# A hybrid decoder layer on one core: the third token chunk's down projection of the first MLP group placed ahead, the second chunk's sums ordered by use, and the first norm's constant moved

## The chip, the cores and the metric

One core of a Trainium2 chip runs the whole layer. The core has a matrix engine (TensorE, PE in the rows; PEld is its weight load), three element-wise engines (VectorE, DVE; ScalarE, ACT; GpSimd, POOL) and a queue that issues transfers (SyncE, SP). The metric is the device time of one execution in microseconds (us), as the median of several runs.

## What is computed

The layer takes 1024 prompt tokens and 8 sampled tokens of width 1024. It norms them, projects them, runs a gated delta rule and a sparse attention, merges the two and adds the residual (h). The MLP behind it takes about two fifths of the time. What matters here, cut from the reference:

```
def rms_norm(x, g):
    y = xf * rsqrt(mean(xf * xf) + EPS);  return y * g
...
xn = rms_norm(x, norm1_g);  ... = split(xn @ w_in)
mix = sigmoid(ga) * (oa @ w_out_a) + sigmoid(gb) * (ob @ w_out_b)
h  = x + mix @ w_o
hn = rms_norm(h, norm2_g)
y  = h + square(relu(hn @ w_up)) @ w_down
```

## The kernel before

Tokens lie along the free dimension in three chunks: 0 and 1 of 384 tokens, 2 of 264 (256 prompt tokens and the 8 samples). `CN` holds the widths. Features lie on the 128 partitions, in 8 slices of 128. Every float32 factor is split into a high and a low part (`split`: ScalarE copies the high part, VectorE or GpSimd subtracts for the low part), and each product is three matmuls, high by high, low by high, high by low.

The program is written as generators ("chains") that `flow.run` interleaves by events (`ev_...`); then a scheduler of the framework puts the instructions of each engine in a fixed order. An engine takes its instructions strictly in that order. All operations are issued through one helper, so every row of the profile shows line 86, and one goes by tile names.

**Start.** `x_chain` loads a tile of 128 tokens (`xt`), gets 1/rms with three small Newton steps on VectorE (`rs`, `ru`), and multiplies tile, 1/rms and the weight `g1`. The Newton steps are written without their usual halves, which leaves a factor of -8192 in `rs`; one GpSimd operation on the 128x1024 weight `g1` takes it out. TensorE then transposes the tile (`ptx`), and `xn` gets the high and low parts. Products `pk` with the weight `wk` (8 slices, split by ScalarE and GpSimd) and `pqi` with `wiq` follow.

**Merge.** For chunks in the order 2, 0 (`FIRST`) and then 1 (`REST`), the attention result `ob` is projected and gated into `mix`, and `mix @ w_o` is added to the residual `hT[j]` in 8 steps (`pdn<-mix,wc`). After each step `part` squares the new slice and adds it to `ssq[j]`.

**Second norm.** `norm_chain` turns the sums of squares into 1/rms (`rs[j]`): a matmul with ones (`pn`), then `rsqrt` (ten VectorE operations, on tiles 264 or 384 wide for chunks 2 and 0; for chunk 1 on 3 columns, which three transposes `pb` widen again). Chunk 2 becomes `hn`, normed and split. Chunks 0 and 1 go through a product scheme that needs seven products of 2x2 blocks instead of eight: with b11, b21 the halves of chunk 0 and b12, b22 those of chunk 1, it forms t1 = b12 - b11, t2 = b22 - t1, t3 = b22 - b12, t4 = b21 - t2 (tiles `bt`; `b22` too is needed in parts), and like sums of weight blocks (`pair`).

**MLP.** `mlp_chain` runs 8 groups `g` of 512 hidden features. A group has products up (`pc` for chunk 2, `pp` for chunks 0 and 1), a squared ReLU (`out`, tiles `r`, `u`), and products down (`pdn<-u,wc`), added to `hT` in 8 steps for chunks 1, 0, 2. In the first group (`g == 0`) all `pc` and the products with b11 and b21 stand ahead of `ev_n[1]`, the end of chunk 1's norm; the products with the `bt` tiles and all of down stand behind it. Weight blocks (128x512, tiles `wc`) are loaded, split and handed out by `ahead` in the order of the list `todo`. `cur["spare"]` names a further raw buffer for every third block.

Of the kernel before, what the change touches and what calls it, by code (L numbers as in the profile page):

```python
# [8 lines left out]
F32 = mybir.dt.float32  # L9
# [7 lines left out]
P = 128  # L17
# [111 lines left out]
def program(ctx, tc, I, O, dbg=None, upto=99):  # L129
# [321 lines left out]
    def mixers():  # L451
# [49 lines left out]
        def x_chain():  # L501
# [12 lines left out]
            G.tensor_scalar(g1, g1, -1.0 / 8192, None, op0=OP.mult)  # L514
            wk = w([P, 2, KT, 336], "wk", F32R)
            for i, t in enumerate(XO):
# [12 lines left out]
                V.scalar_tensor_tensor(x_[:n], x_[:n], z[:n], g1[:n], op0=OP.mult, op1=OP.mult)  # L529
# [1101 lines left out]
    def rest():  # L1631
        M = stage("M")
        cur["c12"] = [(M, 2), (M, 2)] + cur["c12"]
        cur["spare"], cur["hp"] = (M, "raw2", 1), M
# [97 lines left out]
        def pool_chain():  # L1732
# [10 lines left out]
            for j in chunks:  # L1743
                ssq[j], rs[j] = sr[:, 0, cs(j)], sr[:, 1, cs(j)]
            hn[2] = parts("hn2", 2, "hn2", 2)
            flow.set(ev_5)
            yield

        def part(j, m):

            h = hT[j][:, m]
            sq = w([P, CM], "sq", bufs=3, pool=st[5])[:, :CN[j]]
            S.activation(sq if m else ssq[j], h, AF.Square)
            if m:
                (V if j == 1 else G).tensor_tensor(ssq[j], ssq[j], sq, OP.add)

        def normed(out, j, m):
            V.scalar_tensor_tensor(out, hT[j][:, m], g2[:, m:m + 1], rs[j], op0=OP.mult, op1=OP.mult)

        def norm_chain():  # L1760
            yield ev_5
            cur["p"] = st[5]
            for j in FIRST:
                yield ev_o[j]
                for m in range(8):
                    part(j, m)
                    yield
            for j in FIRST:
                pn = pst("pn", "pt")[:, :CN[j]]
                T.matmul(pn, ones, ssq[j], start=True, stop=True)  # L1770
                v = w([P, CM], "v", tag="sq", bufs=3)[:, :CN[j]]
                V.tensor_scalar(v, pn, 1.0 / D, EPS, op0=OP.mult, op1=OP.add)
                rsqrt(rs[j], v, w([P, CM], "rst", tag="sq", bufs=3)[:, :CN[j]])
                yield
                if j == 0:
                    x0 = w([P, 2, 4, CM], "x0", F32, 2, "c12", M).rearrange("p a k n -> p (a k) n")
                    for i in "11", "21":
                        B[i] = w([P, 2, 4, CM], "b" + i, F32R, 2, "bm")
                for m in range(8):
                    if j == 0:  # L1780
                        normed(x0[:, m], j, m)
                        b = B["21" if m > 3 else "11"]
                        split(b[:, 0, m % 4], b[:, 1, m % 4], x0[:, m], "act", "dve")
                    else:
                        xh = w([P, CM], "xh", tag="sq", bufs=3)[:, :CN[j]]
                        normed(xh, j, m)
                        split(hn[2](0, m), hn[2](1, m), xh, "act", "pool")
                    yield
                flow.set(ev_n[j])
                yield  # L1790
            yield ev_h

            pn = pst("pn", "pt")
            for i in range(3):
                T.matmul(pn[:, i:i + 1], ssq[1][:, i * P:(i + 1) * P], ones[:, :1], start=True, stop=True)
# [6 lines left out]
            V.tensor_copy(rs[1], pb[:, :CM])  # L1802
            yield
            for i in "t2", "t1", "t3", "22", "t4":
                B[i] = w([P, 2, 4, CM], "b" + i, F32R, 5, "c12")

            def done(i, k, src, lo):
                split(B[i][:, 0, k], B[i][:, 1, k], src, "act", lo)
# [21 lines left out]
        def mlp_chain():  # L1830
            yield ev_h
            cur["p"] = st[5]
            yield ev_n[2]
            yield ev_n[0]

            def out(u, f, c, q):
# [201 lines left out]
```

## Time and profile before

| | us |
|---|---|
| runs (median of 3, lowest, highest) | 1855.07, 1851.83, 1855.9 |
| profiled execution, its own time | 1850.89 |
| its span, first to last instruction | 1849.1 |
| TensorE busy | 1749.6 (95%) |
| VectorE busy | 1232.9 (67%) |
| ScalarE busy | 831.3 (45%) |
| GpSimd busy | 720.2 (39%) |

Shares are of the span. Busy time of TensorE counts a matmul that runs at half clock or that is drawn out as fully busy, so a stage is read by its number of matmuls and by the clock granted in it.

### The profile page before, as it was taken

Reading aid. Unit: us, or ns where it says so; the run is one execution under the profiler, and the core shown is the slowest. Engines: PE = TensorE matmul, PEld = TensorE weight load, DVE = VectorE, ACT = ScalarE, POOL = GpSimd, SP = SyncE. Lnnn points to the kernel's source line nnn. Section 1 sums busy time; section 2 is a strip of 40 time slices with the busy share of each in tenths; the row PEclk is TensorE's granted clock in tenths of the full one; section 3 lists DMA queues with packets and bytes.
Section 4 is the critical chain, followed back from the end, with each engine's and each line's share of the span. In section 5 each row is a group of like instructions: output and inputs, shape, how many; then the busy total and the mean of one; then the engine's idle time right before and its main releaser. Section 6 shows DMA issues by size and latency. Waiting matters only on the chain.

```text
span 1849.1 us, 32447 instructions
## 1 busy us (share of the span) xinstructions
PE 1749.6 (95%) x11611; PEld 1676.4 (91%) x11611; DVE 1232.9 (67%) x3084; ACT 831.3 (45%) x1927; POOL 720.2 (39%) x824
## 2 busy tenths in 40 slices
PE   6998989799999998989899988799999999999999
PEld 5998979799998888979889877699999999999999
DVE  8876768997888797268889378845354544444452
ACT  5456675466687642245667344413132322223130
POOL 5433236613432345231453394715141433324240
PEclk9999989999999999999999999799999999999999
DMA  6434473314444452663664642102021211111122
GB/s 214 131 104 153 141 223 100 93 58 134 126 142 127 140 155 88 201 219 117 181 172 138 187 134 86 57 29 70 29 69 35 63 40 58 52 40 58 35 63 92
DMA packets 161297, 201.37 MB, mean 109 GB/s; under 512 B 29776, under 2 KB 107592, under 8 KB 161128
## 3 DMA queue, kind: packets, MB, share of 16 engines
q1 hardware_dynamic: 156848, 185.66, 32.5%
q0 software_dynamic: 4288, 13.64, 2.5%
q8 instruction: 91, 1.49, 0.3%
q14 instruction: 70, 0.57, 0.1%
HBM read 151.61 MB, written 47.73 MB: 108 GB/s over the span
## 4 chain that ended last, share of the span: by engine, by line
PE 42%; DVE 4%; POOL 2%; issue 1%; DMA 1%; ACT 0%; SPq 0%; DVEq 0%; POOLq 0%; ACTq 0%
PE pdn L86 23%; PE pp L86 12%; PE pc L86 5%; PE po L86 1%; PE pat L86 1%; PE ptp L86 1%; POOL sr L86 1%; DVE wc L86 1%; DVE b L86 0%; DMA ld<-obd 0%; DVE sr L86 0%; DVE x L86 0%; DVE rst L86 0%; DVE bt L86 0%; POOL wc L86 0%
## 5 line engine op out<-in xcount | busy, mean ns | idle before, releaser
L86 PE MATMUL pdn<-u,wc 128*128 128x384 f32 (+1 forms) x2304 | 361.9, 318 | 0.0
L86 PEld LDWEIGHTS pdn<-u,wc 128*128 128x128 f32 x2304 | 361.2, 188 | 0.0
L86 DVE TENSOR_TENSOR hT<-hT,pdn 128x384 f32<-128x384 f32 (+1 forms) x216 | 110.3, 512 | 221.4 <-PE pdn L86 221.2
L86 PE MATMUL pdn<-xn,wu 128*128 128x384 f32 (+1 forms) x1440 | 251.5, 327 | 0.7 <-ACT z L86 0.7
L86 PEld LDWEIGHTS pdn<-xn,wu 128*128 128x128 f32 x1440 | 228.1, 191 | 7.6 <-issue 3.8
L86 PE MATMUL pp<-bt,wc 128*128 128x384 f32 x768 | 147.4, 345 | 17.5 <-ACT bt L86 11.3
L86 PE MATMUL pa<-xn,wu 128*128 128x384 f32 (+1 forms) x864 | 157.9, 330 | 0.3 <-ACT a L86 0.3
L86 PEld LDWEIGHTS pp<-bt,wc 128*128 128x128 f32 x768 | 137.3, 194 | 21.8 <-ACT bt L86 12.6
L86 PEld LDWEIGHTS pa<-xn,wu 128*128 128x128 f32 x864 | 140.1, 194 | 2.9 <-ACT a L86 1.1
L86 POOL TENSOR_TENSOR u<-r,u 128x384 fp32r<-128x384 f32 (+1 forms) x96 | 104.4, 1098 | 70.5 <-ACT u L86 70.5
L86 ACT ACTIVATE jka<-sc,nf 128x512 bf16<-128x512 f32 (+3 forms) x124 | 101.4, 821 | 40.3 <-DVE nf L86 27.6
L86 PE MATMUL pp<-b,wc 128*128 128x384 f32 x576 | 110.6, 337 | 4.2 <-ACT b L86 3.6
L86 PE MATMUL pdn<-mix,wc 128*128 128x384 f32 (+1 forms) x576 | 97.0, 324 | 9.0 <-DVE wc L86 4.2
L86 PEld LDWEIGHTS pp<-b,wc 128*128 128x128 f32 x576 | 99.7, 189 | 5.2 <-ACT b L86 4.0
L86 PE MATMUL pc<-hn,wc 128*128 128x264 f32 x768 | 104.1, 286 | 0.1
L86 PEld LDWEIGHTS pdn<-mix,wc 128*128 128x128 f32 x576 | 91.8, 190 | 13.5 <-DVE wc L86 5.4
L86 PEld LDWEIGHTS pc<-hn,wc 128*128 128x128 f32 x768 | 100.7, 191 | 0.4 <-DVE wc L86 0.4
L86 ACT ACTIVATE u<-r 128x384 fp32r<-128x384 f32 (+1 forms) x96 | 46.6, 488 | 87.0 <-DVE r L86 86.5
L86 DVE SCALAR_TENSOR_TENSOR a<-u,cw,a 128x384 f32<-128x384 f32 (+1 forms) x108 | 71.4, 663 | 9.1 <-ACT a L86 7.8
L86 POOL TENSOR_TENSOR wu<-wu_4r,wu 128x512 fp32r<-128x512 f32 x32 | 42.1, 1315 | 88.6 <-ACT wu L86 82.2
L86 DVE TENSOR_SCALAR_CACHE_REDUCE jk<-sc,cf 128x768 bf16<-128x768 f32 (+1 forms) x62 | 66.4, 1073 | 1.6 <-ACT jka L86 1.5
L86 DVE SCALAR_TENSOR_TENSOR sc<-rl,wsg,sc 128x512 f32<-128x512 f32 (+1 forms) x70 | 53.7, 769 | 12.5 <-ACT rl L86 11.4
(1037 smaller groups left out, 3719.8 us busy)
## 6 DMA issues: line engine op xcount, KB each, us to landing
wu_0r<-in_w_un SPq DMA_DIRECT2D x32, 256.0 KB
wu_4r<-in_w_un SPq DMA_DIRECT2D x32, 256.0 KB
gd<-g SPq DMA_DIRECT2D x32, 192.0 KB
ga<-gd SPq DMA_DIRECT2D x32, 192.0 KB
cqd<-a SPq DMA_DIRECT2D x24, 192.0 KB
xt<-in_x_prompt SPq DMA_DIRECT2D x8, 512.0 KB
obd<-rb SPq DMA_DIRECT2D x16, 256.0 KB
kvd<-kvt SPq DMA_DIRECT2D x8, 384.0 KB
```

The source lines that it names most:

```text
L86: return f(*a, **k)
```

## The change

Seven things change; what is computed stays the same.

1. First norm: the constant -1/8192 is put into `rs` (one 128x1 operation for each tile) instead of into `g1`. For the first two tiles the multiplication is done in two halves.
2. Chunk 2 is no longer multiplied by 1/rms ahead of the up products: `hn` is `hT` by the norm weight, split (low part on VectorE, before on GpSimd), and `rs[2]`, in a tile of its own, is multiplied in behind them, in `out` (a VectorE operation in place of a ScalarE one, 4 in each group).
3. Chunk 0's 1/rms is found on 3 columns, as chunk 1's was (`rms`), and copied by ScalarE. Its squares are summed on VectorE, before on GpSimd.
4. Chunk 1's sums are made sum by sum (t2, t1, t3, b22, t4), before slice by slice. All low parts are on VectorE, before 12 of 20 on GpSimd.
5. In the first group the down products of chunk 2 (96 matmuls) stand ahead of `ev_n[1]`. The 8 blocks of `w_dn` are loaded and split twice for that.
6. The up blocks of the first group come in the order 0, 2, 3, 1.
7. The spare raw buffer of the attention and merge stage (`raw2`) is gone.

```
@@ x_chain
-            G.tensor_scalar(g1, g1, -1.0 / 8192, None, op0=OP.mult)
...
-                V.scalar_tensor_tensor(x_[:n], x_[:n], z[:n], g1[:n], op0=OP.mult, op1=OP.mult)
+                V.tensor_scalar(z[:n], z[:n], -1.0 / 8192, None, op0=OP.mult)
+                for c in (slice(0, 512), slice(512, D)) if i < 2 else (slice(0, D),):
+                    V.scalar_tensor_tensor(x_[:n, c], x_[:n, c], z[:n], g1[:n, c], op0=OP.mult, op1=OP.mult)
@@ rest
-        cur["spare"], cur["hp"] = (M, "raw2", 1), M
+        cur["hp"] = M
...
+            rs[2] = w([P, CN[2]], "rs2")
...
+        def square(j, m, eng):
+            sq = w([P, CM], "sq", bufs=3, pool=st[5])[:, :CN[j]]
+            S.activation(sq if m else ssq[j], hT[j][:, m], AF.Square)
+            if m:
+                eng.tensor_tensor(ssq[j], ssq[j], sq, OP.add)
...
+        def done(i, k, src):
+            split(B[i][:, 0, k], B[i][:, 1, k], src, "act", "dve")
+        def rms(j):
...
+            copy("act", rs[j], pb[:, :CM])
+        def norm_chain():
...
+            yield ev_o[2]
+            for m in range(8):
+                h = hT[2][:, m]
+                S.activation(hn[2](0, m), h, AF.Copy, scale=g2[:, m:m + 1])
+                V.scalar_tensor_tensor(hn[2](1, m), h, g2[:, m:m + 1], hn[2](0, m).bitcast(F32), op0=OP.mult, op1=OP.subtract)
+                square(2, m, G)
+                yield
...
+            yield ev_o[0]
+            for m in range(8):
+                square(0, m, V)
+                yield
+            rms(0)
...
+            yield ev_h
+            rms(1)
+            yield
+            x1 = w([P, 2, 4, CM], "x1", F32, 5, "c12").rearrange("p a k n -> p (a k) n")
+            for i in "t2", "t1", "t3", "22":
                 B[i] = w([P, 2, 4, CM], "b" + i, F32R, 5, "c12")
...
             for k in range(4):
+                normed(x1[:, k], 1, k)
+                normed(x1[:, k + 4], 1, k + 4)
+                V.tensor_tensor(x0[:, k], x1[:, k], x0[:, k], OP.subtract)
+                t2 = w([P, CM], "t2", tag="sq", bufs=3)
+                V.tensor_tensor(t2, x1[:, k + 4], x0[:, k], OP.subtract)
+                done("t2", k, t2)
                 G.tensor_tensor(x0[:, k + 4], x0[:, k + 4], t2, OP.subtract)
+                yield
+            for k in range(4):
+                done("t1", k, x0[:, k])
...
+                V.tensor_tensor(x1[:, k], x1[:, k + 4], x1[:, k], OP.subtract)
+                done("t3", k, x1[:, k])
...
+                done("22", k, x1[:, k + 4])
...
+                done("t4", k, x0[:, k + 4])
             flow.set(ev_n[1])
@@ mlp_chain
-            yield ev_n[2]
             yield ev_n[0]
...
                 if q is None:
-                    S.activation(r, c, AF.Relu)
+                    V.scalar_tensor_tensor(r, c, 0.0, rs[2], op0=OP.max, op1=OP.mult)
                     S.activation(r, r, AF.Square)
...
+                        for i in (0, 2) if not f else (2, 0):
...
+                    yield from down([2])
                     yield ev_n[1]
...
+                yield from down((1, 0, 2) if g else (1, 0))
...
-    todo += [b for f in (0, 2, 1, 3) for b in halves(I["w_up"][f])]
+    todo += [b for f in (0, 2, 3, 1) for b in halves(I["w_up"][f])] + [I["w_dn"][0, m] for m in range(8)]
```

The scheduler's order shows the change at three places. First VectorE at the very start: `xt` is the token tile, `rs` its 1/rms, `ss` the sum of squares of the second tile. A piece of the difference:

```order
 L86 SCALAR_TENSOR_TENSOR ru<-rs,ss 128x1
 L86 SCALAR_TENSOR_TENSOR rs<-ru,rs 128x1
+L86 TENSOR_SCALAR rs<-rs 128x1
+L86 SCALAR_TENSOR_TENSOR xt<-xt,rs,g_135 128x512 x2
 L86 TENSOR_SCALAR ss<-ss 128x1
 L86 TENSOR_SCALAR rs<-ss 128x1
```

The first tile's multiplication now stands ahead of the second tile's Newton steps; before, it stood behind five of them. The order on all engines is the same again some sixty microseconds later, and stays so up to the attention stage.

Second TensorE in the first group, after the last `mix` product. Before (`bt_14498` is t2, `bt_14499` t1, `bt_14500` t3, `b_14501` b22):

```order
L86 MATMUL pc<-hn_13649,wc_14598 128x264 x12
L86 MATMUL pp<-bt_14498,wc_14661 128x384
L86 MATMUL pp<-bt_14499,wc_14694 128x384
L86 MATMUL pp<-bt_14498,wc_14661 128x384 x2
L86 MATMUL pp<-bt_14500,wc_14711 128x384
L86 MATMUL pp<-b_14501,wc_14773 128x384
L86 MATMUL pp<-bt_14499,wc_14694 128x384 x2
```

And of the change (`u_14466` is chunk 2's squared ReLU; the weights 14614, 14637, 14677, 14720 and 14739 are the first five of the eight down blocks):

```order
L86 MATMUL pp<-b_13948,wc_14597 128x384 x12
L86 MATMUL pdn<-u_14466,wc_14614 128x264
L86 MATMUL pdn<-u_14466,wc_14637 128x264
L86 MATMUL pdn<-u_14466,wc_14677 128x264
L86 MATMUL pdn<-u_14466,wc_14614 128x264 x2
L86 MATMUL pdn<-u_14466,wc_14637 128x264 x2
L86 MATMUL pdn<-u_14466,wc_14677 128x264 x2
L86 MATMUL pdn<-u_14466,wc_14720 128x264 x3
L86 MATMUL pdn<-u_14466,wc_14739 128x264 x3
L86 MATMUL pdn<-u_14466,wc_14614 128x264
```

The 96 down matmuls of chunk 2 now stand between the last product with b21 and the first with t2. They begin with the three of the first hidden slice for five blocks (15 matmuls); the remaining 81 read the other three slices.

Third VectorE in the same place. Before (`b` and `t` are slices, `x` holds t1 and later t4):

```order
L86 SCALAR_TENSOR_TENSOR b_14630<-hT_13973,g_116,sr 128x384
L86 TENSOR_TENSOR t_14505<-b_14504,x_14076 128x384
L86 TENSOR_TENSOR b_14503<-b_14504,b_14503 128x384
L86 TENSOR_TENSOR x_14076<-b_14630,x_14076 128x384
L86 TENSOR_TENSOR bt_14498<-t_14505,bt_14498 128x384
L86 TENSOR_TENSOR b_14630<-b_14631,b_14630 128x384
L86 TENSOR_TENSOR bt_14499<-x_14076,bt_14499 128x384
```

And of the change (`bt_14501` is t2, `bt_14502` t1, `bt_14503` t3, `b_14504` b22; `r<-pc` is the ReLU of chunk 2, four in all, of which the first stands ahead of these rows):

```order
L86 TENSOR_TENSOR bt_14502<-x_13946,bt_14502 128x384 x4
L86 TENSOR_TENSOR bt_14503<-x_14500,bt_14503 128x384
L86 SCALAR_TENSOR_TENSOR r<-pc,rs_13658 128x264
L86 TENSOR_TENSOR b_14504<-x_14500,b_14504 128x384 x4
L86 TENSOR_TENSOR bt_14501<-t_14569,bt_14501 128x384
L86 TENSOR_TENSOR bt_14503<-x_14500,bt_14503 128x384 x3
L86 SCALAR_TENSOR_TENSOR r<-pc,rs_13658 128x264
L86 TENSOR_TENSOR t_14672<-x_14500,x_13946 128x384
L86 SCALAR_TENSOR_TENSOR r<-pc,rs_13658 128x264
L86 TENSOR_TENSOR bt_14501<-t_14672,bt_14501 128x384
```

VectorE now makes whole sums one after another, and the last two ReLUs of chunk 2, which the down products above need, stand near the end of that list.

## Rows read from the trace of the kernel before

**Rows 1.** Windows: busy us and count (x) of each engine, PE clock, DMA.

```profile
0.00:20.00 20.00, 2.56 (x10) 1.97 (x11) 12.73 (x23) 9.96 (x19) 14.91 (x33) 1.00 0.87 282
...
1080.00:1124.00 44.00, 37.97 (x199) 35.43 (x199) 40.03 (x54) 17.06 (x35) 32.69 (x27) 0.96 0.39 123
1123.69:1150.90 27.21, 23.52 (x154) 22.63 (x153) 21.70 (x44) 11.53 (x25) 8.95 (x6) 0.94 0.24 78
1150.90:1199.57 48.67, 30.52 (x122) 25.84 (x122) 42.68 (x54) 20.42 (x45) 37.96 (x30) 0.79 0.15 49
1199.57:1244.79 45.22, 45.22 (x290) 45.20 (x290) 22.09 (x37) 7.00 (x12) 10.55 (x9) 1.00 0.10 30
1244.79:1330.67 85.88, 85.88 (x553) 85.88 (x553) 39.98 (x66) 23.32 (x46) 29.31 (x24) 1.00 0.17 50
```

**Rows 2.** Chain that ended last, in order of time: start, us, what ran.

```profile
1246.89 1.46 PE pc L86 x12
1248.35 8.32 PE pp L86 x48
```

**Rows 3.** Waits of TensorE, 1090 to 1200 us.

```profile
PE pp L86 <- ACT bt L86: 11.3, 4, 8.6
PE pp L86 <- DVE bt L86: 5.7, 4, 3.3
PE pdn L86 <- DVE wc L86: 4.0, 2, 3.6
PE pp L86 <- ACT b L86: 3.6, 2, 1.9
```

**Rows 4.** Timeline of TensorE around the first group: start, us, what.

```profile
1148.57 2.33 PE L86 MATMUL pc<-hn,wc 128*128 128x264 f32 x17
1159.53 2.18 PE L86 MATMUL pp<-bt,wc 128*128 128x384 f32 x5 [8.62 <-ACT bt L86]
...
1185.39 10.18 PE L86 MATMUL pp<-bt,wc 128*128 128x384 f32 x43 [0.63 <-DVE bt L86]
```

**Rows 5.** Timeline of VectorE, chunk 1's norm and sums.

```profile
1143.47 0.15 DVE L86 TENSOR_SCALAR v<-pn 128x3 f32<-128x3 f32 x1
...
1149.00 0.55 DVE L86 COPY sr<-pb 128x384 f32<-128x384 f32 x1
...
1158.84 0.55 DVE L86 TENSOR_TENSOR b<-b,b 128x384 f32<-128x384 f32 x1
1159.31 0.55 DVE L86 TENSOR_TENSOR x<-b,x 128x384 f32<-128x384 f32 x1
...
1167.28 1.35 DVE L86 TENSOR_TENSOR b<-b,b 128x384 f32<-128x384 f32 x1
1168.56 1.35 DVE L86 TENSOR_TENSOR bt<-b,bt 128x384 fp32r<-128x384 f32 x1
```

**Rows 6.** Timeline of ScalarE, chunk 2's squared ReLU, high part.

```profile
1155.06 0.42 ACT L86 ACTIVATE u<-r 128x264 fp32r<-128x264 f32 x1
```

**Rows 7.** Timeline of GpSimd, same stretch.

```profile
1155.56 0.74 POOL L86 TENSOR_TENSOR u<-r,u 128x264 fp32r<-128x264 f32 x1 [1.41 <-ACT u L86]
...
1168.18 2.59 POOL L86 TENSOR_TENSOR bt<-x,bt 128x384 fp32r<-128x384 f32 x2
```

**Rows 8.** Timeline of VectorE, start of the kernel.

```profile
7.98 0.16 DVE L86 SCALAR_TENSOR_TENSOR rs<-ru,rs 128x1 f32<-128x1 f32 x1
...
12.08 2.00 DVE L86 SCALAR_TENSOR_TENSOR xt<-xt,rs,g 128x1024 f32<-128x1024 f32 x1
```

**Rows 9.** Timeline of GpSimd, start of the kernel.

```profile
6.18 2.80 POOL L86 TENSOR_SCALAR g<-g 128x1024 f32<-128x1024 f32 x1 [2.88 <-DMA g<-in_norm_g]
10.39 5.29 POOL L86 TENSOR_TENSOR wk<-wkr,wk 128x336 fp32r<-128x336 f32 x5 [1.41 <-ACT wk L86]
...
25.29 1.81 POOL L86 TENSOR_TENSOR wk<-wkr,wk 128x336 fp32r<-128x336 f32 x2 [1.25 <-ACT wk L86]
```

**Rows 10.** Waits of TensorE, 780 to 1100 us: ScalarE's weight split.

```profile
PE pdn L86 <- ACT wc L86: 1.5, 2, 0.7
```

More of the change, by code (lines that the diff above doesn't have):

```diff
@@ L1747, in pool_chain @@
             yield
-        def part(j, m):
[L1751 to L1791, printed above, removed]
@@ L1825, in norm_chain @@
+            yield
+            for k in range(4):
+                V.tensor_tensor(x1[:, k], x1[:, k + 4], x1[:, k], OP.subtract)
+                done("t3", k, x1[:, k])
+            yield
+            for k in range(4):
+                done("22", k, x1[:, k + 4])
+            yield
+            B["t4"] = w([P, 2, 4, CM], "bt4", F32R, 5, "c12")
+            for k in range(4):
+                done("t4", k, x0[:, k + 4])
             flow.set(ev_n[1])
@@ L1873, in mlp_chain, with down, ev @@
                 held = {}
+                def down(js):
+                    for m in range(8):
+                        def ev(j, c, p):
+                            V.tensor_tensor(hT[j][:, m], hT[j][:, m], p, OP.add)
+                            if g == 7:
+                                dma(O["yT"][:, m, c], hT[j][:, m])
+                        yield from dense(blocks(1), lambda a, k, j: u[j][:, a, k], ev, js)
                 if g == 0:
                     for f in range(2):
-                        pc = [pst("pc", "pd")[:, :CN[2]] for _ in range(2)]
-                        ws = blocks(1)
-                        prod(pc[0], ws, hn2(0), True, False)
-                        yield
-                        p1 = copied(full(ws, "11"))
-                        yield
-                        ws = blocks(1)
-                        prod(pc[0], ws, hn2(1), False)
-                        out(u[2], f, pc[0], None)
-                        yield
-                        held[f] = p1, full(ws, "21")
-                        yield
-                        for h in range(2):
-                            prod(pc[1], blocks(1), hn2(h), h == 0, h == 1)
-                        out(u[2], f + 2, pc[1], None)
-                        yield
+                        for i in (0, 2) if not f else (2, 0):
+                            pc = pst("pc", "pd")[:, :CN[2]]
+                            ws = blocks(1)
+                            prod(pc, ws, hn2(0), True, False)
+                            if not i:
+                                p1 = copied(full(ws, "11"))
+                            yield
+                            ws = blocks(1)
+                            prod(pc, ws, hn2(1), False)
+                            out(u[2], f + i, pc, None)
+                            if not i:
+                                held[f] = p1, full(ws, "21")
+                            yield
+                    yield from down([2])
                     yield ev_n[1]
@@ L1929, in mlp_chain @@
                     yield
-                for m in range(8):
-                    def ev(j, c, p):
-                        V.tensor_tensor(hT[j][:, m], hT[j][:, m], p, OP.add)
-                        if g == 7:
-                            dma(O["yT"][:, m, c], hT[j][:, m])
-                    yield from dense(blocks(1), lambda a, k, j: u[j][:, a, k], ev, (1, 0, 2))
+                yield from down((1, 0, 2) if g else (1, 0))
         flow.run([value_chain(), logit_chain(), pool_chain(), merge_chain(), norm_chain(), mlp_chain()], cur)
```

38 lines of the change are left out of this document (19 added, 19 removed).

## The prediction

> **What bounds the kernel now.** I read the busy shares first, then the chain that ended last, then TensorE by windows, then the orders of VectorE and GpSimd where TensorE stands still.
>
> The second half is TensorE without a gap. From 1199.57 us on TensorE is busy all the time at full clock, and each later group takes 85.88 us [rows 1]. In such a group 12 products of 264 columns take 1.46 us and 12 of 384 columns 8.32/4 = 2.08 us [rows 2], so one product is 0.122 or 0.173 us. Nothing in the change lowers the number of these products; in that half only standing still can be removed, and there is none. So what the change can win lies ahead of 1199.57 us, and every microsecond won there arrives at the end.
>
> There are three places. (a) The start: the first tile is multiplied only at 12.08 us, and TensorE has 2.56 us of work in the first 20 [rows 1, 8]. (b) Chunk 1's merge, 1080 to 1123.69 us: TensorE is busy 37.97 of 44 us at a mean clock of 0.96 [rows 1]; its 192 `mix` products are 192 x 0.173 = 33.3 us, begun at 1080.2, so about 10 of 43.5 us are lost. (c) The first group. Call T0 the end of the last `mix` product, 1123.69 us. The group's products are those of any group, 85.9 us, and it ends at 1244.79, 121.1 us after T0: 35.2 us are lost. Of these 48.67 - 10 x 2.08 = 27.9 lie between 1150.90 and 1199.57, where TensorE waits for the `bt` tiles (11.3 and 5.7 us [rows 3]) and then runs at a clock of 0.79; the other 7.2 lie ahead of it, among them 3.6 us of waiting for `b` [rows 1, 3].
>
> **The change, part by part.**
>
> *Start.* 1/rms is ready at 7.98 + 0.16 = 8.14 us; the weight's scaling on GpSimd ends at 8.98, and the tile's multiplication, put behind the second tile's steps, ends at 14.08 [rows 8, 9]. After the change a 128x1 operation (0.16) and the first half (at most 2.00/2) follow, so the transposes can start at 9.3, 4.8 us earlier. That is the upper bound. The lower bound is nothing: `pk` also needs GpSimd's low parts of `wk`, of which five are done at 15.68 and the last at 27.10 [rows 9], and GpSimd began them only at 10.39, when its 2.80 us of scaling had long ended; with the scaling gone they need not come earlier. I take 3 us, since VectorE's list for the second tile moves up by nearly 4 and the `wk` blocks behind the fifth wait for buffers that free with it. The nine added 128x1 operations (9 x 0.16 = 1.4 us) are spread over 50 us. As the order stays the same up to the attention stage, I let the 3 us run through.
>
> *Attention and merge.* One raw buffer less for every third of some 40 weight blocks. TensorE waits for ScalarE's weight split twice there, 1.5 us in all [rows 10], so the cover is thin, but there. The scheduler also reorders the stage. I take 0, from -4 to +4.
>
> *Merge of chunk 1.* VectorE is busy 40.03 of 44 us and GpSimd 32.69 [rows 1], and one wait of TensorE for a weight part on VectorE is 3.6 us long [rows 3]. Gone are chunk 0's wide `rsqrt` (eleven operations 384 wide, now eleven at 0.15), eight `xh`, and on GpSimd seven sums of squares and eight low parts; added on VectorE are seven sums. That is some 19 wide operations against 7. Of the 10 us lost I take half back, 5, between 0 and 10.
>
> *First group.* What TensorE has ahead of the down products: 96 products `pc` (8 x 1.46 = 11.7 us), 48 with b11 and b21 (8.3) and the small `pn` and `pb` (1.2): it arrives there at T0 + 21.2. I assume no wait for `b`, since chunk 0's 1/rms comes without the wide `rsqrt`. The next 15 products read only u's first slice (1.8 us). The other 81 need the slice whose ReLU is last on VectorE.
>
> When is that? The last add to `hT`, its square and its sum end about 3.3 us behind T0; `pn` stands in TensorE's order behind 41 products and comes at T0 + 5.9; eleven 128x3 operations and one weight part follow to T0 + 9.4; `pb` stands behind 43 more products, T0 + 12.1, and the copy ends at T0 + 13.3. Before, the stretch from the first of these operations to the copy took 1143.47 to 1149.55, 6.1 us [rows 5]; here 6.7. Then VectorE has, up to the fourth `r<-pc`, 33 operations of 384 columns, 4 of 264 and 2 weight parts. Undisturbed, 384-wide operations follow each other at 1159.31 - 1158.84 = 0.47 us; while GpSimd works, at 1168.56 - 1167.28 = 1.28 us [rows 5, 7]. Undisturbed the list is 33 x 0.47 + 4 x 0.4 + 2 x 0.6 = 18.3 us. GpSimd has some five operations in it, each of about 1.3 us (2.59 for two [rows 7]) and each holding up one of VectorE's by 0.8: 4 us. So the last `r` is there at T0 + 35.6, and after a square and a high part on ScalarE (0.42 each [rows 6]) TensorE goes on at T0 + 36.4; the low part on GpSimd takes 0.74 more [rows 7], beside the first products. TensorE has then waited 36.4 - 21.2 - 1.8 = 13.4 us.
>
> The Trainium skill bears on the 0.8 us: SBUF — State Buffer, "Who interferes with whom", says that a VectorE instruction with two SBUF inputs and a GpSimd instruction that reads SBUF exclude each other for a whole instruction. By that rule each of the five would cost up to its full 1.3 us and the wait would be 2.5 us longer; the trace's alternation at 1.28 us agrees with the kind of it.
>
> The long wait also costs clock. Before, five products behind the 8.62 us wait took 2.18 us, 0.44 each, and the 43 from 1185.39 on took 10.18 us for 7.4 [rows 4], 2.7 over. I take 3.5 here. Chunk 1's sums are all made by then, since VectorE makes t1, t3 and b22 ahead of the last `r`; t2 and t4 end within 3 us and the 81 products cover them. For weight blocks that arrive late among the 10 products I take 1.5. Lost after T0: 13.4 + 3.5 + 1.5 = 18.4, against 35.2. Won: 16.8. Bounds: with GpSimd's five operations not felt and the clock back at once, 18.4 - 4 - 2.5 = 12 lost, 23 won; with every third of the 33 operations held up (11 x 0.8 in place of 4) and 6 us of clock, 26 lost, 9 won.
>
> *The later groups.* ScalarE gives 4 operations to VectorE in each, about 4 x 0.4 us; VectorE is busy 39.98 of 85.88 us [rows 1], and `pc` has free PSUM tiles. If that cover were gone it would cost up to 11 us over seven groups. The second split of eight `w_dn` blocks falls where ScalarE and GpSimd are less than half busy. Nothing for both.
>
> *Sum.* 3 + 0 + 5 + 16.8 = 24.8 us from the profiled execution's own 1850.89: 1826. The runs' median lies 4.2 above that execution, at 1855.07, so I name 1830.
>
> **The rivals.**
>
> *A, chunk 2's last slice is later still.* The constants behind T0 or the contention are worse, and the first group wins 9 or less; with 1 from the start and 2 from the merge the time is 1843. For it: before, VectorE ran at the contended pace in this list, as at 1167 to 1169 [rows 5]. Against: 12 of GpSimd's low parts are gone from there.
>
> *B, the down products wait little.* VectorE's list runs undisturbed and starts earlier, because the adds of the merge no longer queue; 23 from the group, 8 from the merge, 4 from the start: 1820.
>
> *C, the change does not do what it says at the start.* `wk` on GpSimd holds `pk` where it was, and the merge's loss is in its loads: only the group's 16.8 remain, 1838.
>
> *D, slower.* The missing raw buffer makes the weights late through the attention and merge stage. The price is one wait like those of 0.7 us [rows 10] for each block; with the 24.8 us won elsewhere it decides from 24.8/40 = 0.62 us for each of the 40 blocks, and at 0.75 each the time would be 1855 + 5 = 1860. Against: only two such waits show now, and blocks at 2.08 us of products each leave four buffers some 8 us of lead.
>
> **How the numbers follow.** My forecast, 1830 within 6 us either way, has 0.47; A 0.18, B 0.12, C 0.14, D 0.05; the 0.04 left is a reordering of the attention stage that eats the gain to within 0.2%, 3.7 us, which is about what a measurement of this kernel can tell from no change. A, B, C and the forecast are all faster: 0.91. Slower is D, 0.05, same 0.04. From 1818 to 1847 the range holds the forecast, B and C and most of A, and leaves out D, the lost gain and the tails, under 2 in 10.
>
> **What would show each step.** Right: the first transposes near 9 us; in the merge no wait for `wc` of several us; after the products with b21 a wait of TensorE of about 13 us for `u`, released by ScalarE or GpSimd, and behind it the ten `bt` products with hardly a wait; the first group 103 us long from the last `mix` product, later groups 85.9. Wrong: TensorE waiting for `bt` again, for `wc` in the attention stage, or VectorE's list at 1.28 us a piece; or a first 40 us in which TensorE does no more products than now.

## The result, and the profile after

| | before | changed |
|---|---|---|
| median of the runs shown | 1853.51 us (4 runs) | 1832.83 us (4 runs) |
| ratio, 95% interval | | 0.9885 [0.9862, 0.9908] |
| span of the profiled execution | 1849.1 us | 1829.9 us |
| its own time | 1850.89 us | 1831.62 us |
| T0, the end of the last `mix` product | 1123.69 us | 1121.04 us |
| first product of the second group | 1244.62 us | 1225.97 us |
| the first group, from T0 to that product | 120.9 us | 104.9 us |

The change is faster by 1.15%; 1830 us was forecast. The medians lie 20.7 us apart, where 24.8 were forecast. The 19.2 us between the two spans are 2.65 up to T0, 16.0 in the first group, and 7 x 0.08 in the seven later ones. In the windows below (columns as in [rows 1]) a later group takes 85.80 us against 85.88 in [rows 1].

```profile
1121.04:1142.30 21.26, 21.23 (x154) 20.91 (x153) 15.80 (x36) 7.03 (x13) 6.78 (x5) 1.00 0.31 95
1142.30:1158.62 16.32, 4.56 (x16) 3.55 (x16) 15.97 (x28) 9.89 (x24) 7.57 (x7) 0.59 0.08 28
1158.62:1170.40 11.78, 11.76 (x82) 11.45 (x82) 10.01 (x18) 5.71 (x11) 5.45 (x6) 0.85 0.12 45
1170.40:1191.20 20.80, 20.80 (x123) 20.80 (x121) 19.88 (x30) 8.11 (x16) 13.87 (x11) 1.00 0.49 152
1191.20:1225.97 34.77, 33.89 (x193) 33.16 (x193) 19.77 (x29) 6.99 (x12) 11.02 (x9) 1.00 0.14 39
1225.97:1311.77 85.80, 85.80 (x553) 85.80 (x553) 42.83 (x70) 22.32 (x42) 29.56 (x24) 1.00 0.17 50
```

TensorE in the first group (start, us, what, and in brackets the idle time before it and what ended it):

```profile
1149.46 0.81 PE L86 MATMUL pdn<-u,wc 128*128 128x264 f32 x2 [7.18 <-ACT u L86]
1151.87 1.91 PE L86 MATMUL pdn<-u,wc 128*128 128x264 f32 x7 [1.61 <-DVE r L86]
1156.51 1.84 PE L86 MATMUL pdn<-u,wc 128*128 128x264 f32 x6 [2.73 <-DVE r L86]
1158.62 11.94 PE L86 MATMUL pdn<-u,wc 128*128 128x264 f32 x81 [0.26 <-ACT u L86]
1170.40 6.40 PE L86 MATMUL pp<-bt,wc 128*128 128x384 f32 x36
...
1225.97 2.26 PE L86 MATMUL pp<-b,wc 128*128 128x384 f32 x12
```

The place of the wait has moved. The 3.6 us for `b` and the 11.3 and 5.7 us for `bt` of [rows 3] are gone; TensorE reaches the third chunk's down products at 1142.28 us, T0 + 21.2, and waits 7.18, 1.61, 2.73 and 0.26 us for u and for r, the ReLU that u is made of. The last 81 products begin at T0 + 37.6. Behind them the ten products with `bt` and b take 20.80 us, 10 x 2.08, without a gap. So of the 16.0 us won in the group 6.0 lie ahead of this place (21.2 us from T0, against 27.2 before in [rows 1]) and 10.0 behind it.

VectorE in the same stretch, then ScalarE:

```profile
1142.40 0.42 DVE L86 SCALAR_TENSOR_TENSOR r<-pc,rs 128x264 f32<-128x264 f32 x1
...
1143.95 1.35 DVE L86 TENSOR_TENSOR t<-x,x 128x384 f32<-128x384 f32 x1
...
1151.40 0.42 DVE L86 SCALAR_TENSOR_TENSOR r<-pc,rs 128x264 f32<-128x264 f32 x1
...
1156.04 0.42 DVE L86 SCALAR_TENSOR_TENSOR r<-pc,rs 128x264 f32<-128x264 f32 x1
...
1156.85 0.42 DVE L86 SCALAR_TENSOR_TENSOR r<-pc,rs 128x264 f32<-128x264 f32 x1
```

```profile
1149.00 0.41 ACT L86 ACTIVATE u<-r 128x264 fp32r<-128x264 f32 x1
```

The first slice's r is taken from `pc` only at 1142.40, although its products had ended by 1130; the other three follow at 1151.40, 1156.04 and 1156.85, between operations for the sums. VectorE is not the only one: the first slice's r is ready at 1142.82, but u is made of it on ScalarE only at 1149.00, behind high parts of the sums in ScalarE's list. That ends the wait of 7.18 us. The last wait, behind which 81 of the 96 products stand, ends with the fourth r, the one of 1156.85.

The start: VectorE, then TensorE.

```profile
7.98 1.42 DVE L86 SCALAR_TENSOR_TENSOR xt<-xt,rs,g 128x512 f32<-128x512 f32 x2
...
10.53 0.80 DVE L86 SCALAR_TENSOR_TENSOR rs<-ru,rs 128x1 f32<-128x1 f32 x1
...
24.05 1.28 DVE L86 SCALAR_TENSOR_TENSOR xt<-xt,rs,g 128x1024 f32<-128x1024 f32 x1
```

```profile
8.78 1.97 PE L86 MATMUL ptx<-ident,xt 128*128 128x128 f32 x8 [8.78 <-DVE xt L86]
...
40.51 2.16 PE L86 MATMUL pk<-wk,xn 128*128 128x336 f32 x13
```

The first half tile is done early and the first transposes begin at 8.78 us, against 14.13 before, when the multiplication only began at 12.08 [rows 8]. But the 128x1 steps of the second tile's norm take 0.8 us each while GpSimd works, and the third tile's multiplication begins at 24.05 us (24.10 before). The third tile's first `pk` product, at 40.51, is 0.7 us ahead (41.19 before). In the nine executions here whose kernel is the changed one up to T0 (all but before, e4, e6, e8 and e9) it begins at 40.2 to 42.1 us, on the mean at 40.9; in the three with the old start (before, e4 and e9) at 41.2 to 42.3, on the mean at 41.6. Of the lead of 5.3 us, 0.7 is left there, less than the scatter.

### The profile page after: what moved, and what is told of

It reads as the page before. It is cut to its first block, busy times and chain, and to the rows that moved or that the text cites. A ratio compares the mean times of both kernels' runs of the same rounds, so it can differ in the third digit from the quotient of the medians.

```text
span 1829.9 us, 32566 instructions
## 1 busy us (share of the span) xinstructions
PE 1743.9 (95%) x11618; PEld 1676.5 (92%) x11618; DVE 1256.6 (69%) x3149; ACT 826.6 (45%) x1905; POOL 691.2 (38%) x800
## 5 line engine op out<-in xcount | busy, mean ns | idle before, releaser
L86 PE MATMUL pdn<-u,wc 128*128 128x384 f32 (+1 forms) x2304 | 366.5, 320 | 12.7 <-ACT u L86 7.8
L86 PE MATMUL pp<-bt,wc 128*128 128x384 f32 x768 | 138.3, 336 | 0.0
L86 POOL TENSOR_TENSOR u<-r,u 128x384 fp32r<-128x384 f32 (+1 forms) x96 | 108.4, 1140 | 71.2 <-ACT u L86 70.7
L86 PEld LDWEIGHTS pp<-bt,wc 128*128 128x128 f32 x768 | 132.8, 188 | 0.0
L86 POOL TENSOR_TENSOR wu<-wu_4r,wu 128x512 fp32r<-128x512 f32 x32 | 41.6, 1301 | 87.9 <-ACT wu L86 81.5
```

The costliest lines, as they stand in the source:

```text
L86: return f(*a, **k)
```

## The experiments

All profiled executions by the same marks; the group is the stretch from T0 to the second group's first product. Each ratio is to runs of the kernel before that were taken beside it (medians 1853.51, 1853.07, 1852.16 and 1851.13 us).

| kernel | median, us (ratio to before, 95%) | T0 | group |
|---|---|---|---|
| before | | 1123.69 | 120.9 |
| changed | 1832.83 (0.9885 [0.9862, 0.9908]) | 1121.04 | 104.9 |
| e1 down products not ahead | 1837.01 (0.9916 [0.9894, 0.9938]) | 1122.18 | 107.9 |
| e2 r in own buffers | 1829.02 (0.9878 [0.9860, 0.9896]) | 1119.94 | 102.9 |
| e3 r's product on GpSimd | 1841.28 (0.9935 [0.9917, 0.9953]) | 1128.29 | 112.6 |
| e4 first norm as before | 1833.50 (one run) | 1122.59 | 105.1 |
| e5 no low parts of the sums | 1829.06 (one run) | 1124.11 | 98.7 |
| e6 third norm before | 1836.52 (0.9926 [0.9907, 0.9946]) | 1121.02 | 105.4 |
| e7 x0's sums on VectorE | 1831.54 (one run) | 1120.12 | 105.6 |
| e8 wk's low parts on VectorE | 1832.98 (0.9906 [0.9879, 0.9934]) | 1119.18 | 105.1 |
| e9 down products ahead alone | 1852.99 (1.0012 [1.0001, 1.0022]) | 1125.05 | 120.9 |
| e10 one weight part on GpSimd | 1827.94 (0.9872 [0.9852, 0.9893]) | 1119.09 | 103.4 |
| e11 changed, again | 1829.99 (0.9887 [0.9867, 0.9907]) | 1118.80 | 104.9 |
| e12 e2, again | 1830.61 (0.9883 [0.9863, 0.9903]) | 1123.81 | 102.8 |

The group's length repeats to 0.1 us (changed and e11, e2 and e12). T0 doesn't: it moves by 2.2 and 3.9 us between two executions of one kernel. So the group is read from the traces, and a few us ahead of T0 can't be read from one trace.

**e1: the third chunk's down products back behind the others.**

```
-                    yield from down([2])
                     yield ev_n[1]
...
-                yield from down((1, 0, 2) if g else (1, 0))
+                yield from down((1, 0, 2))
...
-    todo += [b for f in (0, 2, 3, 1) for b in halves(I["w_up"][f])] + [I["w_dn"][0, m] for m in range(8)]
+    todo += [b for f in (0, 2, 3, 1) for b in halves(I["w_up"][f])]
```

> The changed kernel with the third chunk's down products of the first group put back behind the other two chunks' (and its 8 w_dn blocks loaded once). T0 is the end of the last mix product. Theory A (the prediction's): these 96 products (11.7 us) are what TensorE does while VectorE makes the sums; without them it waits from T0+21.2 until the last bt of the sum for t2 is there, T0+38 to T0+41 by the trace of the changed kernel; less its first 9 products of t2 that is 16 to 18 us of waiting where the changed kernel waits 11.8: slower than the changed kernel by 4 to 6 us, 1836 to 1838 us. Rival B (the products stand in no gap, since the first of them waits for VectorE just as long): within 1 us of the changed kernel, 1831 to 1834. Rival C (the whole cover of 11.7 us is lost): 1843 to 1845.

TensorE in e1:

```profile
1148.20 1.10 PE L86 MATMUL pp<-bt,wc 128*128 128x384 f32 x2 [4.79 <-ACT bt L86]
1154.63 4.23 PE L86 MATMUL pp<-bt,wc 128*128 128x384 f32 x14 [5.33 <-DVE bt L86]
```

The group is 3.0 us longer than in the changed kernel. TensorE waits 4.79 and 5.33 us for the first `bt`, and some 4.6 us more later. Theory A had the direction, but too large a size: 14.7 us of waiting where it had 16 to 18, and 3.0 us where it had 4 to 6 (the median, 1837.01, lies within its range). Of 16 us won in the group, 13 are there without the products ahead. 6.0 of the 13 lie ahead of the first product with `bt`, where chunk 0's new norm leaves no wait for `b`; 7.0 lie behind it. No run takes the order of the sums and the engine of their low parts apart.

**e9: the other half alone,** the products ahead in the kernel before, with its norm and sums.

```
+                    yield from down([2])
                     yield ev_n[1]
...
+                yield from down((1, 0, 2) if g else (1, 0))
...
-    todo += [b for f in (0, 2, 1, 3) for b in halves(I["w_up"][f])]
+    todo += [b for f in (0, 2, 1, 3) for b in halves(I["w_up"][f])] + [I["w_dn"][0, m] for m in range(8)]
```

> The kernel before with one part of the change alone: the third chunk's down products of the first group go ahead of the wait for the second chunk's sums (its 8 w_dn blocks loaded twice); norm, sums, start and the third ring of raw blocks as before. The other half alone (e1) gave the first group a length of 107.9 us from T0, against 121.1 before and 105.0 in the changed kernel. Theory A (the two halves hide the same wait, so that they don't add): down products ahead cover most of their 11.7 us, less what u waits for on GpSimd, which has 16 low parts of the sums to make there: the group is 109 to 114 us long, 1841 to 1847 us. Rival B (they add: the changed kernel less e1 is all that the products ahead are worth): 118 us, about 1850 us.

TensorE in e9, then VectorE:

```profile
1157.82 1.03 PE L86 MATMUL pdn<-u,wc 128*128 128x264 f32 x3 [2.63 <-ACT r L86]
...
1168.29 7.63 PE L86 MATMUL pdn<-u,wc 128*128 128x264 f32 x40 [2.08 <-POOL u L86]
1181.21 1.66 PE L86 MATMUL pdn<-u,wc 128*128 128x264 f32 x6 [5.30 <-DVE hT L86]
...
1245.97 2.24 PE L86 MATMUL pp<-b,wc 128*128 128x384 f32 x12
```

```profile
1172.16 1.36 DVE L86 TENSOR_TENSOR bt<-x,bt 128x384 fp32r<-128x384 f32 x1
1173.44 1.36 DVE L86 TENSOR_TENSOR bt<-t,bt 128x384 fp32r<-128x384 f32 x1
...
1180.65 1.43 DVE L86 TENSOR_TENSOR hT<-hT,pdn 128x264 f32<-128x264 f32 x4
```

Nothing at all: 120.9 us, as before. The products stand in the gap, but they wait there as `bt` did: 11.2 us for r and u, which ScalarE and GpSimd make here among their parts of the sums, then 5.30 us for the additions to `hT` on VectorE, whose queue still goes at 1.28 us an operation. r shares its buffers with a tile of the sums here too (`sq`); buffers of its own were not tried with the old sums. The two halves don't add by themselves: the products ahead are worth 0.0 us with the old sums and 3.0 with the new ones. Both forecasts failed: theory A's 109 to 114 us by 7 or more, rival B's 118 by 3.

**e2: the same operations, r in buffers of its own.**

```
-                r = w([P, CM], "r", tag="sq", bufs=3)[:, :n]
+                r = (w([P, CM], "r", tag="gb", bufs=3, pool=M) if q is None and not g
+                     else w([P, CM], "r", tag="sq", bufs=3))[:, :n]
```

> The changed kernel, but r of the third chunk's four slices in the first group lies in the three buffers of gb, which are idle there, not in the three of sq, which the sums t2 use as well; no operation is added or taken away. Theory A (the prediction's: r is late since VectorE has about 37 operations of the norm and the sums to do, whatever their buffers): the waits of TensorE for u and r stay at 10 to 12 us, time 1830 to 1834. Theory B (r is late since it shares buffers with t2, which puts it behind t2 in VectorE's order; with its own it stands ahead of the normed tiles): the first wait of 7.2 us goes, the waits for u and r together are 2 to 6 us, and the bt products wait 0 to 3 us in their place: 1824 to 1829.

VectorE in e2, then TensorE:

```profile
1125.15 0.43 DVE L86 SCALAR_TENSOR_TENSOR r<-pc,rs 128x264 f32<-128x264 f32 x1
...
1130.84 0.43 DVE L86 SCALAR_TENSOR_TENSOR r<-pc,rs 128x264 f32<-128x264 f32 x1 [1.24 <-PE pc L86]
...
1138.42 0.41 DVE L86 SCALAR_TENSOR_TENSOR r<-pc,rs 128x264 f32<-128x264 f32 x1
...
1142.18 0.41 DVE L86 SCALAR_TENSOR_TENSOR r<-pc,rs 128x264 f32<-128x264 f32 x1
...
1148.58 0.68 DVE L86 TENSOR_TENSOR wc<-wc92r,wc 128x512 fp32r<-128x512 f32 x1
```

```profile
1143.44 0.63 PE L86 MATMUL pdn<-u,wc 128*128 128x264 f32 x3 [0.94 <-POOL wc L86]
1149.31 8.56 PE L86 MATMUL pdn<-u,wc 128*128 128x264 f32 x46 [5.24 <-DVE wc L86]
...
1163.15 3.19 PE L86 MATMUL pdn<-u,wc 128*128 128x264 f32 x22 [1.17 <-DVE hT L86]
```

Both theories were half right. The buffers did decide where r stands: with its own, three of the four stand ahead of the sums, and the wait for u and r is gone. But TensorE now waits 0.94, 5.24, 0.40, 1.50 and 1.17 us, 9.3 in all against 11.8, for weight blocks and additions to `hT`. The longest is for the low part that VectorE makes at 1148.58, behind the sums. The releaser's name changed, and 2.0 us were won.

**e10: that one block's low part on GpSimd,** on top of e2.

```
-                lo = "pool" if i % 2 else "dve"
+                lo = "pool" if i % 2 or i in (92,) else "dve"
```

> e2, with the low part of one weight block (the one for which TensorE waits 5.24 us in e2, its fifth of w_dn) on GpSimd in place of VectorE. Theory A (TensorE is held by the queue of VectorE and GpSimd as a whole, and what it is said to wait for is only what stands last there): that wait falls to 1 to 4 us, but the next thing in the queue, u of slice 1 (made at T0+29 to T0+30.5), is waited for in its place; the group is 101 to 103 us long (102.9 in e2). Rival B (the place of that one block is the whole cost): 97.5 to 99 us, 1824 to 1825 us.

TensorE in e10:

```profile
1142.60 0.63 PE L86 MATMUL pdn<-u,wc 128*128 128x264 f32 x3 [0.94 <-POOL wc L86]
1146.44 0.59 PE L86 MATMUL pdn<-u,wc 128*128 128x264 f32 x1 [3.22 <-POOL wc L86]
1149.00 8.32 PE L86 MATMUL pdn<-u,wc 128*128 128x264 f32 x45 [1.97 <-ACT u L86]
```

The 5.24 us become 3.22 for that block, on GpSimd now, and 1.97 for u behind it: 5.19 together. That is theory A's mechanism; the group, 103.4 us, came out just over its 101 to 103. Rival B's 97.5 to 99 is out.

**e5: 20 operations off VectorE,** on top of e2.

```
 def done(i, k, src):
-    split(B[i][:, 0, k], B[i][:, 1, k], src, "act", "dve")
+    if i in ("11", "21"):
+        split(B[i][:, 0, k], B[i][:, 1, k], src, "act", "dve")
+    else:
+        copy("act", B[i][:, 0, k], src)
...
-                        T.matmul(p, wk[:, i], b[:, a, k] if not callable(b) else b(a, k), ...)
+                        T.matmul(p, wk[:, i], b[:, a if any(b is B[x] for x in ("11", "21")) else 0, k] if not callable(b) else b(a, k), ...)
```

> e2, with the low parts of the second chunk's sums t2, t1, t3, t4 and of 22 left out: 20 VectorE subtractions of about 0.47 us are gone, and the products that read these low parts read the high part in their place, so that TensorE's work is the same (the output is not the reference's in the last bits). In e2 the first group is 102.9 us long from T0 and TensorE waits 9.2 us in its 96 down products of the third chunk, mostly for weight blocks whose low part stands behind the sums on VectorE. Theory A (VectorE's queue is the bound, whoever is named as the releaser): 9.4 us less work there, so the waits fall under 2 us and the group is 95 to 97 us long. Rival B (the weight blocks are late for another reason, their buffers, transfers or GpSimd): waits of 7 us or more, group 101 to 103 us.

(The result changes by more than the last bits that the expectation names: the high part's product counts twice. TensorE's work is the same.) TensorE in e5:

```profile
1147.60 0.63 PE L86 MATMUL pdn<-u,wc 128*128 128x264 f32 x3 [0.93 <-POOL wc L86]
1153.47 0.59 PE L86 MATMUL pdn<-u,wc 128*128 128x264 f32 x1 [5.23 <-DVE wc L86]
1154.80 12.34 PE L86 MATMUL pdn<-u,wc 128*128 128x264 f32 x81 [0.75 <-ACT u L86]
```

The group is 98.7 us, 4.2 shorter than in e2, though 9.4 us of VectorE's time were gone. The waits in the 96 down products fall from 9.3 to 6.9 us, and those products themselves take 14.9 us in place of 16.0; the other 0.8 us lie behind them. Neither forecast came: the waits are far over theory A's 2 us, the group is shorter than rival B's 101. The 0.94 and 5.24 stay as 0.93 and 5.23, since these low parts stood behind that block in VectorE's order; all but 0.75 us of what waited behind them is gone. So VectorE's queue is the bound up to each thing waited for, not as a sum.

**e3: r's product with 1/rms on GpSimd** (all groups; buffers as in the changed kernel).

```
-                    V.scalar_tensor_tensor(r, c, 0.0, rs[2], op0=OP.max, op1=OP.mult)
+                    S.activation(r, c, AF.Relu)
+                    G.tensor_tensor(r, r, rs[2], OP.mult)
```

> The changed kernel, but r of the third chunk is made by a ReLU on ScalarE from PSUM and its product with 1/rms on GpSimd, in place of one VectorE operation, in all 8 groups, with the buffers as they are. Theory A (VectorE's list sets the wait): the last r is no longer behind 33 operations of VectorE; the waits for u and r fall from 11.8 us to under 5, time 1822 to 1828. Theory B (the shared buffers of r and t2 set it): r is as late as before, now on ScalarE, and one GpSimd operation of about 0.75 to 1.0 us is put into each slice's chain: waits of 11 to 15 us, time 1831 to 1836. In the later groups both expect nothing (under 0.2 us a group).

```profile
1156.48 0.81 PE L86 MATMUL pdn<-u,wc 128*128 128x264 f32 x2 [6.95 <-ACT u L86]
...
1161.30 1.69 PE L86 MATMUL pdn<-u,wc 128*128 128x264 f32 x6 [2.56 <-ACT r L86]
1166.75 1.03 PE L86 MATMUL pdn<-u,wc 128*128 128x264 f32 x3 [3.76 <-ACT r L86]
1171.31 12.79 PE L86 MATMUL pdn<-u,wc 128*128 128x264 f32 x81 [3.53 <-ACT u L86]
```

```profile
1147.10 6.10 POOL L86 TENSOR_TENSOR wc<-wc91r,wc 128x512 fp32r<-128x512 f32 x1 [4.43 <-ACT wc L86]
1153.16 0.74 POOL L86 TENSOR_TENSOR r<-r,rs 128x264 f32<-128x264 f32 x1
```

Above is TensorE in e3, then GpSimd. The waits grow to 17.0 us (with 0.20 between those shown), the group to 112.6, 7.6 more than in the changed kernel. ScalarE does take the first r from `pc` earlier, at 1146.92, T0 + 18.6; but its product with 1/rms comes only at 1153.16, since GpSimd's operation ahead of it, a weight's low part, stood for 6.10 us. So the first wait is not the shared buffers' doing here; it is the link through GpSimd, and what holds GpSimd up. Theory B's direction, at well over its price, and for the first slice another cause.

**e6: the third chunk normed ahead, as before the change,** on top of e2: `hn` gets 1/rms, r is a ReLU on ScalarE.

```
-                S.activation(hn[2](0, m), h, AF.Copy, scale=g2[:, m:m + 1])
-                V.scalar_tensor_tensor(hn[2](1, m), h, g2[:, m:m + 1], ...)
...
+                normed(xh, 2, m)
+                split(hn[2](0, m), hn[2](1, m), xh, "act", "pool")
...
-                    V.scalar_tensor_tensor(r, c, 0.0, rs[2], op0=OP.max, op1=OP.mult)
+                    S.activation(r, c, AF.Relu)
```

> e2, with the third chunk normed into hn ahead of its products as in the kernel before (so that r is a ReLU on ScalarE, with its own buffers): four VectorE operations of 0.42 us leave the first group, eight normed operations on VectorE and eight low parts on GpSimd go into the merge of the second chunk. Theory A (VectorE's queue is the bound): TensorE's waits in the group fall from 9.2 us by about 1.7, the group is 100.5 to 102 us long, and the merge gives 0 to 2 us back: 1827 to 1830 us. Rival B (what counts is who shares buffers and stands where in an engine's order): the wait moves to u on ScalarE again, group 104 us or more, 1831 to 1835 us.

TensorE in e6:

```profile
1142.10 8.90 PE L86 MATMUL pdn<-u,wc 128*128 128x264 f32 x72
...
1164.60 1.65 PE L86 MATMUL pp<-bt,wc 128*128 128x384 f32 x4 [5.75 <-ACT wc L86]
1169.21 8.51 PE L86 MATMUL pp<-bt,wc 128*128 128x384 f32 x32 [2.96 <-POOL wc L86]
```

72 of the down products now run unbroken, the other 24 wait 2.9 us, and as much time as was saved is lost behind them: 5.75 and 2.96 us for the next weight blocks, whose sums stand in VectorE's queue. The group is 105.4 us, and chunk 1's merge, 1073.41 to T0, 47.6 (42.6 in the changed kernel). Rival B's length of the group came, by theory A's mechanism; the median, 1836.5, is above the range of both.

**e7: the four subtractions from x0 on VectorE,** on top of e2.

```
-                G.tensor_tensor(x0[:, k + 4], x0[:, k + 4], t2, OP.subtract)
+                V.tensor_tensor(x0[:, k + 4], x0[:, k + 4], t2, OP.subtract)
```

> e2, with the four subtractions x0 minus t2 on VectorE in place of GpSimd. The prediction priced a GpSimd operation of 128x384 among VectorE's at 0.8 us of VectorE's time, against 0.47 us for doing it there. Theory A (a GpSimd operation holds VectorE up for about its own length): four times 0.33 less, the group is 101 to 102.5 us long (102.9 in e2). Rival B (GpSimd holds VectorE up by nothing): four times 0.47 more, 104 to 105.5 us.

TensorE in e7, then GpSimd:

```profile
1147.54 0.59 PE L86 MATMUL pdn<-u,wc 128*128 128x264 f32 x1 [3.28 <-DVE wc L86]
...
1156.58 12.20 PE L86 MATMUL pdn<-u,wc 128*128 128x264 f32 x76 [6.13 <-POOL u L86]
```

```profile
1138.91 4.66 POOL L86 TENSOR_TENSOR wc<-wc91r,wc 128x512 fp32r<-128x512 f32 x1 [4.35 <-ACT wc L86]
...
1149.01 7.51 POOL L86 TENSOR_TENSOR u<-r,u 128x264 fp32r<-128x264 f32 x1 [4.41 <-ACT u L86]
```

The group is 105.6 us, but for neither reason given. VectorE's queue did get shorter (5.24 became 3.28). Then one GpSimd operation, u's low part, took 7.51 us in place of 0.74 [rows 7], and VectorE ran from 1148.35 to 1155.92 without a pause on sums of two tiles in SBUF; TensorE waited 6.13 us for it. So this run says nothing of the 0.8 us that it was made to test.

**e4 and e8: the start.** e4 has the first norm as before; e8 makes the low parts of `wk` on VectorE.

```
-                        split(wk[:, 0, k], wk[:, 1, k], raw, "act", "pool")
+                        split(wk[:, 0, k], wk[:, 1, k], raw, "act", "dve")
```

> The changed kernel with the first norm as it was (constant on GpSimd over 128x1024, whole tiles of x_). The prediction's term: the start's gain of 3 us lasts, so this ends the attention stage 3 us later than the changed kernel. Rival C: the lead is lost within the first 40 us, since the transfers are at over nine tenths until about 25 us and the third tile of x lands at 17.2 in both kernels: the third tile's pk products begin at 40.5 to 41.5 us, the first mix products of the attention stage's end at 1020 to 1021 us as in both, and the group gains all that the changed kernel gains, own time within 2 us of 1832.

> The changed kernel with the low parts of w_kv's eight blocks at the start made by VectorE in place of GpSimd (eight operations of 128x336). In the changed kernel the first transposes begin at 8.78 us, against 14.13 before, but the third tile of x's pk products of the program (its second group of tiles) begin at 40.51, against 41.19 before; between 10.5 and 27 us VectorE's 128x1 operations of the norm take 0.8 us in place of 0.15 to 0.22 while GpSimd makes the low parts of wk and wiq. Theory A (the lead is lost since GpSimd's operations hold up the norm's chain on VectorE): the 128x1 operations between 10.4 and 14.8 us fall to 0.15 to 0.35 us, and those pk products begin at 37 to 39.5 us. Rival B (transfers: the DMA engines are over nine tenths busy until about 25 us, and the third tile of x lands at 17.2 in both kernels): 40 to 41 us as now. In both the time is within 2 us of the changed kernel's 1832.8 unless the lead lasts to the end of the attention stage, where the mix products begin at 1020.0 in the changed kernel.

In e4 the `mix` products begin at 1020.37 us (1020.03 in the changed kernel), T0 is 1122.59 and the group 105.1 us: nothing of 3 us, within the scatter of T0. One run alone could not exclude 3 us; the means over all executions, in the section above and the next, are the better evidence. In e8 most of the 128x1 steps between 10.4 and 15.3 fall to 0.15 to 0.22 us, as theory A wanted, yet the marked `pk` begins at 41.62, within the scatter of the others and not at 37 to 39.5. VectorE now has the low parts itself, and the second tile's multiplication begins no earlier (15.29 us, 14.99 in the changed kernel), so theory A's forecast fails, but the contention is not excluded as a part of the cause. The third tile of x is used by ScalarE at 17.25 us in the changed kernel, 17.27 in e8 and 17.30 before, which is rival B's first half; that an earlier transfer would keep the lead was not tried.

**e11 and e12: the changed kernel and e2 side by side.**

> The changed kernel once more beside e12, for a direct comparison: ratio 0.986 to 0.991, first group 105 us from T0. Up to the last mix product its time is not of the change (the same orders of instructions): the start of the mix products should scatter by 1 to 3 us about 1020.

> e2 once more beside e11. By the group's length (102.9 against 105.0 us) its median should be 1 to 3 us under that of e11; if the group was only luckily short in that one execution, the medians are within 1 us and the group here is 104 to 105.5 us long.

The group's 2.1 us repeat; the medians, 1829.99 and 1830.61, don't show them. In the two profiled executions T0 alone lies 5.0 us apart, later in e12. Neither e2 nor e10 can be told from the changed kernel by time.

## Why the prediction was right

Sign, size and mechanism of the main term hold. The two smaller terms, 8 of the 24.8 us, came as next to nothing, as rival C had it. Of the 20.7 us between the medians the MLP's groups account for 16.6; the other 4 lie in the stretch up to T0, which scatters by several us from one execution to the next. That 1832.8 came this near to 1830 is in part luck.

*First group, 16.8 forecast: 16.0.* T0 + 21.2 for the down products, T0 + 5.9 for `pn` and T0 + 12.1 for `pb` (12.18) came as worked out. VectorE's list began at T0 + 13.4 and ended with the last r at T0 + 36.2, 22.8 us where 22.3 were forecast, without a pause; over the 18.3 undisturbed that is 4.5 us for six operations of GpSimd, about the 0.8 each that was taken, and not 1.3. The last products began at T0 + 37.6, not 36.4. The first 15 products were to go through in 1.8 us behind no wait; they had three waits of their own, since u's slices arrived one by one and the first was held on ScalarE. So the wait of 13.4 us came as 11.8 in four pieces. The clock, 3.5 us in the sum, came as 4.6: the 15 products took 4.56 us for 1.8, at a mean granted clock of 0.59 with the waits, and the 81 took 11.8 for 9.9. The misses partly cancel: 11.8 + 4.6 and the two items that follow make 19.1 us lost after T0, against 18.4 forecast. The 1.5 us for late weights among the ten products came as nothing, while 1.5 us were lost in the two other chunks' down products (34.77 us in the window above, for 192 x 0.173 = 33.3), which had no term. `pn` and `pb`, 1.2 us, stood in the walk but not in the 18.4 of losses.

*What earned it* is a point that the sum alone can't show. I counted the products ahead as the cover and the shorter queue of VectorE as what makes the wait end. e9 and e1 put the weight on the rest of the change: norm and sums are worth 13 us alone, 6.0 of them ahead of the first product with `bt`; the cover alone nothing. The list of 33 operations at 0.47 us rested on these 12 low parts being gone; with them, in the kernel before, it goes at 1.28 us [rows 5], and there the cover waits as well.

*The last r sets the wait.* It did in the changed kernel, but its place in VectorE's list came from its buffers (e2); freed of it, TensorE stands for the next thing, mostly in the same queue. This doesn't change the forecast, only what one would do next.

*Start, 3 forecast.* Rival C's first half was right: the lead is 0.7 us on the mean at 40 us. The `mix` products begin on the mean at 1020.6 us in the nine executions (1016.3 to 1026.8) and at 1021.1 in the three with the old start (1020.4 to 1022.4): 0.5 us, far under the scatter. The step that failed is "I let the 3 us run through".

*Merge, 5 forecast.* From chunk 1's first `mix` product to T0 it is 43.5 us before, 42.6 in the changed kernel, 43.6 in e11, 43.7 in e12 and in e9: 0 to 1. Operations left VectorE there, but TensorE still waits for `wc` (on VectorE's low parts 3.2 us in all in the changed kernel, 4.2 before). The step "I take half back" failed, and that is rival C's other half; what else holds the merge was not tried. T0 is on the mean 1121.9 in the nine executions whose kernel is the changed one up to there, and 1124.4 in before and e9: 2.5 us for start, attention and merge together, where 8 were forecast, and the nine alone run from 1118.8 to 1128.3.

*Attention and rival D.* The stretch was taken as 0. From 780 us to T0 TensorE waits 4.9 us for weight parts in the changed kernel and 6.2 before, so no row shows weights made late by the missing raw buffer. Giving the buffer back was not tried.

*Later groups, nothing forecast:* 85.80 against 85.88 us. Rivals A and B lie 10 us above and 13 below.

## What to carry to other kernels

Work put into a wait fills it only if its own inputs don't stand among the operations that are being waited for: the products ahead needed r, u, weight parts and additions from the three engines that made the sums, and alone they won nothing. A releaser named in a trace is the thing that stood last; before it is moved, list what stands behind it, on that engine first, for that can be the next wait. And of two parts of a change, run each alone: here all the rest is worth 13 us and the products ahead nothing without it.

## What the hardware showed that I had not expected

A single GpSimd operation can stand through a whole run of VectorE's: 7.51 us for one of 0.74 (e7), and for a weight's low part, 1.29 us elsewhere in e7, 4.66 there and 6.10 in e3. I had priced GpSimd by what it takes from VectorE, 0.8 us an operation; in e3 and e7 the larger cost was the other way round. The Trainium skill, SBUF — State Buffer, "Who interferes with whom", says that a VectorE instruction with two SBUF inputs contends with a GpSimd instruction that reads SBUF, and calls the port pair that they share an exclusive lock. The traces agree with the exclusion, and e7 adds that a run of such VectorE instructions, one behind the other, kept GpSimd out for the length of the run. It need not: in e2 the same operation took its 0.74 us inside such a run, which went on from 1148.58 to past 1157 us without a pause:

```profile
1149.60 0.74 POOL L86 TENSOR_TENSOR u<-r,u 128x264 fp32r<-128x264 f32 x1 [1.36 <-ACT u L86]
```

What decides which of the two happens was not looked for.

The granted clock was 0.59 over 1142.30 to 1158.62, where TensorE worked 4.56 of 16.32 us, still 0.85 over the next 11.8 us, in which it never stopped, and 1.00 from there on: so part of that stretch too was at the lower of the two levels, 1.2 GHz, although the wait was over.

Two executions of one kernel reached T0 up to 3.9 us apart and then needed the same time to 0.1 us. The cause of that scatter was not looked for.
